# Strassen's seven products for 16 of the 22 blocks of the down projection, and 13 low halves moved to VectorE

## The chip, the core and the metric

One core of a Trainium2 chip runs the kernel: TensorE (PE) multiplies matrices into eight banks of PSUM, VectorE (DVE), ScalarE (ACT) and GpSimd (POOL) work elementwise, SyncE (SP) issues most of the loads. The metric is the time of one execution on the device in microseconds, the median of several runs. Lower is better.

## The reference

One layer of an encoder with 512 tokens, d_model 1024 and a feed-forward width of 2816, in float32. Two kinds of attention, gates, an output projection w_o and a residual come first; what the change touches is mostly the end:

```python
merged = g_a * (y_a @ w_up_a[l]) + g_b * (y_b @ w_up_b[l])
x = x + gate1[:, None] * (merged @ w_o[l])
h2 = rms_norm(x, norm2_g[l]) * (1.0 + scale2[:, None]) + shift2[:, None]
ff = (jax.nn.silu(h2 @ w_ff1[l]) * (h2 @ w_ff3[l])) @ w_ff2[l]
x = x + gate2[:, None] * ff
```

## The kernel before

**Precision.** Each float32 operand is split into a high half, rounded to the format that TensorE reads (`cp`, a cast on ScalarE, L432), and a low half, the difference (`sb` on VectorE, L456, or `psub` on POOL, L504). A product takes three matmuls: high by high, high by low, low by high (`three`, L519). A matmul has a stationary block of 128 x 128 and up to 512 moving columns.

**Weights** come in units of 128 x 1024 (512 KB): `g` (gates), `up`, `o` (w_o), `f1`, `f3` (one block of 128 columns of w_ff1 or w_ff3) and `f2` (128 rows of w_ff2). A unit is loaded into one of four `raw` buffers, cast into one of three `whi` buffers, and its low half goes into one of three `wlo`. A `raw` buffer is free again when the low half is formed, a `whi` and `wlo` when TensorE has used the unit. `take(u)` prepares units two ahead of the one used (LA = 2). The table `ON_DVE` says whose low halves VectorE forms; `g` and `up` units are not in it and go to POOL.

**Stages.** The units `g` and `up`, mixed with the attention, give the merged input of w_o, each of its eight blocks split into `mh` and `ml`; at the same time loads of the modulation weights (`in_adat`) are multiplied with the condition vector on VectorE (`raw<-raw,cs`, L476). Then come w_o, the second norm and 22 blocks of the feed-forward: for block j, f1 and f3 are multiplied with h2 (48 matmuls of 512 columns, blocks 0 and 1 in two parts), ScalarE takes silu of the one, VectorE multiplies by the other, and the result is split into `f` high and low. After that the 22 f2 units are multiplied into eight banks, `ob[t, h]` for four blocks of 128 tokens and two halves of the output columns: 16 units one after another, then the last six for one bank after the other, so that the outputs leave in turn. The last bank is done in two halves of 256 columns; the first 16 units of its second half are put aside in `first`.

**Order.** `Order.plan` lists every operation with its costs, buffers and priorities and writes out one fixed order for each engine; each engine then runs its instructions strictly in that order and waits on semaphores. A change of any part can move instructions elsewhere. The 36 tiles `t` of 512 columns hold the eight tiles of the residual (`x2`) and, before, the split blocks f.

## Time and profile before

| | us |
|---|---|
| median of 3 runs | 797.6 |
| lowest and highest | 796.84, 798.5 |
| the profiled execution | 797.95 |
| its span, first to last instruction | 795.7 |
| TensorE busy | 781.7 |
| VectorE, ScalarE, POOL busy | 459.3, 350.1, 178.1 |

The profiled execution's own time is 2.25 us more than its span, which lies around the instructions. Matmuls overlap at their ends, so a group's mean is longer than the time from one start to the next. Rows name L of the kernel that was run; an idle time stands in brackets, with what ended it.

### The profile page before, as it was taken

Reading aid. Unit: us, or ns where it says so; the run is one execution under the profiler, and the core shown is the slowest. Engines: PE = TensorE matmul, PEld = TensorE weight load, DVE = VectorE, ACT = ScalarE, POOL = GpSimd, SP = SyncE. Lnnn points to the kernel's source line nnn. Section 1 sums busy time; section 2 is a strip of 40 time slices with the busy share of each in tenths; the row PEclk is TensorE's granted clock in tenths of the full one; section 3 lists DMA queues with packets and bytes.
Section 4 is the critical chain, followed back from the end, with each engine's and each line's share of the span. In section 5 each row is a group of like instructions: output and inputs, shape, how many; then the busy total and the mean of one; then the engine's idle time right before and its main releaser. Section 6 shows DMA issues by size and latency. Waiting matters only on the chain.

```text
span 795.7 us, 11113 instructions
## 1 busy us (share of the span) xinstructions
PE 781.7 (98%) x4275; PEld 673.5 (85%) x4275; DVE 459.3 (58%) x911; ACT 350.1 (44%) x650; POOL 178.1 (22%) x115
## 2 busy tenths in 40 slices
PE   8999999999999999999899999999999999999998
PEld 5988988999899888888588988888888888888886
DVE  6969999765469886778746433443433333212343
ACT  6576575456568767525344332232332322211310
POOL 1056544786565313542001000000000000000000
PEclk9999999999999999999999999999999999999999
DMA  9932121222242333776602223444422232232311
GB/s 347 396 142 81 57 78 54 80 83 78 79 131 83 107 105 93 258 257 221 216 14 80 88 98 127 135 135 158 140 100 100 86 106 95 90 107 90 122 40 66
DMA packets 29147, 97.97 MB, mean 123 GB/s; under 512 B 3235, under 2 KB 4771, under 8 KB 29094
## 3 DMA queue, kind: packets, MB, share of 16 engines
q1 hardware_dynamic: 28518, 96.35, 35.3%
q10 hardware_dynamic: 576, 0.92, 0.3%
q8 instruction: 33, 0.54, 0.3%
q14 instruction: 20, 0.16, 0.1%
HBM read 95.16 MB, written 2.10 MB: 122 GB/s over the span
## 4 chain that ended last, share of the span: by engine, by line
PE 78%; DVE 12%; DMA 4%; ACT 3%; issue 2%; POOL 0%; SPq 0%; ACTq 0%; DVEq 0%; POOLq 0%
PE ff L519 45%; PE gate L519 6%; PE wo L519 4%; PE kb L519 3%; DMA raw<-in_adat 3%; PE qa L519 3%; PE ka L519 3%; DVE sc L878 2%; PE va L519 2%; PE qb L519 2%; PE S L519 2%; DVE m L877 2%; DVE raw L476 2%; PE PT L532 2%; PE idx L519 2%
## 5 line engine op out<-in xcount | busy, mean ns | idle before, releaser
L432 ACT CAST whi<-raw 128x1024 fp32r<-128x1024 f32 x109 | 114.5, 1052 | 279.8 <-PE ff L519 149.0
L456 DVE TENSOR_TENSOR wlo<-raw,whi 128x1024 fp32r<-128x1024 f32 x65 | 79.6, 1224 | 116.1 <-ACT whi L432 113.3
L504 POOL TENSOR_TENSOR wlo<-raw,whi 128x1024 fp32r<-128x1024 f32 x44 | 110.3, 2509 | 157.4 <-ACT whi L432 143.3
L519 PE MATMUL ff<-h2h,wlo 128*128 128x512 f32 (+1 forms) x384 | 142.6, 372 | 0.0
L519 PE MATMUL ff<-h2l,whi 128*128 128x512 f32 (+1 forms) x384 | 142.4, 371 | 0.0
L519 PE MATMUL ff<-h2h,whi 128*128 128x512 f32 (+1 forms) x384 | 142.4, 371 | 0.0
L519 PE MATMUL ff<-whi,f 128*128 128x512 f32 (+1 forms) x310 | 95.2, 385 | 0.0
L519 PEld LDWEIGHTS ff<-h2h,wlo 128*128 128x128 f32 x384 | 72.3, 188 | 12.6
L519 PEld LDWEIGHTS ff<-h2l,whi 128*128 128x128 f32 x384 | 72.3, 188 | 12.5
L519 PEld LDWEIGHTS ff<-h2h,whi 128*128 128x128 f32 x384 | 72.3, 188 | 12.4
L519 PEld LDWEIGHTS ff<-whi,f 128*128 128x128 f32 x310 | 57.9, 188 | 11.6
L519 PE MATMUL ff<-wlo,f 128*128 128x512 f32 (+1 forms) x155 | 59.7, 385 | 0.0
L462 DVE TENSOR_TENSOR silu<-ff,silu 128x512 f32<-128x512 f32 x22 | 15.2, 692 | 70.2 <-PE ff L519 70.2
L476 DVE CUSTOM_DVE_ANT_0 raw<-raw,cs 128x1024 f32<-128x1024 f32 x32 | 45.1, 1422 | 13.0 <-DMA raw<-in_adat 13.0
L519 PE MATMUL gate<-hl,whi 128*128 128x512 f32 x128 | 51.1, 399 | 0.0
L519 PE MATMUL gate<-hh,whi 128*128 128x512 f32 x128 | 51.0, 399 | 0.0
L519 PE MATMUL gate<-hh,wlo 128*128 128x512 f32 x128 | 51.0, 398 | 0.0
L485 POOL TENSOR_TENSOR r<-v,mhalf 128x16 f32<-128x16 f32 (+2 forms) x14 | 29.1, 2080 | 71.5 <-DVE v L466 71.1
L441 ACT ACTIVATE sx<-sx,nm 128x128 f32<-128x128 f32 (+3 forms) x64 | 35.7, 560 | 9.7 <-DVE nm L476 9.5
L519 PEld LDWEIGHTS ff<-wlo,f 128*128 128x128 f32 x155 | 29.1, 188 | 5.9
L519 PE MATMUL wo<-wo,mh 128*128 128x512 f32 x96 | 30.5, 395 | 3.4 <-ACT mh L432 3.4
L470 DVE SCALAR_TENSOR_TENSOR acc<-raw,csc,acc 128x1024 f32<-128x1024 f32 x16 | 20.5, 1279 | 21.3 <-DMA raw<-in_adar 21.2
(229 smaller groups left out, 1692.6 us busy)
## 6 DMA issues: line engine op xcount, KB each, us to landing
raw<-in_wun SPq DMA_DIRECT2D x118, 512.0 KB, 3.3
raw<-in_adat SPq DMA_DIRECT2D x32, 512.0 KB, 7.3
raw<-in_adar SPq DMA_DIRECT2D x16, 512.0 KB, 3.2
x<-in_x SPq DMA_DIRECT2D x4, 512.0 KB, 5.4
praw<-in_wun SPq DMA_DIRECT2D x8, 256.0 KB, 7.4
xr<-in_x SPq DMA_DIRECT2D x4, 512.0 KB, 5.1
praw<-in_wun SPq DMA_DIRECT2D x8, 162.0 KB, 7.4
out_y<-out SPq DMA_DIRECT2D x4, 256.0 KB, 2.0
```

The lines of the kernel that those rows point to most:

```text
L432: nc.scalar.copy(g(o), g(i))
L441: nc.scalar.activation(g(o), g(i), f, scale=g(scale), **kw)
L456: dve(n, False, lambda: nc.vector.tensor_sub(g(o), g(i), g(j)), (i, j), (o,), two=(i, j))
L462: dve(n, False, lambda: nc.vector.tensor_mul(g(o), g(i), g(j)), (i, j), (o,), two=(i, j))
L470: dve(n, False, lambda: nc.vector.scalar_tensor_tensor(g(o), g(i), g(s), g(j), op0=op0, op1=op1), (i, s, j), (o,), len(refs(s)), (i, j))
L476: dve(n, False, lambda: nc.vector.tensor_tensor_reduce(g(o), g(i), g(j), scale, init, op0, op1, g(acc)), (i, j), (o, acc), two=(i, j))
L485: G.op("POOL", 300 + 165 * m, lambda: nc.gpsimd.tensor_tensor(g(o), g(i), g(mhalf[:, 0:1].spread([P, m])), op=ALU.pow), refs(i, mhalf), re ...
L504: G.op("POOL", 147 + 2.106 * n, lambda: nc.gpsimd.tensor_sub(g(o.r()), g(i), g(hi)), (i, hi), (o,), port=True)
L519: lambda: nc.tensor.matmul(g(ap), g(lhsT.r()), g(rhs.r()), start=i == 0, stop=i == self.count - 1), refs(lhsT, rhs), (ap,))
L532: G.op("PE", 109, lambda: nc.tensor.transpose(g(ap), g(in_), g(idt)), refs(in_, idt), (ap,))
L877: dve(n, False, lambda: nc.vector.max(g(m8), g(s)), (s,), (m8,))
L878: dve(n, False, lambda: nc.vector.match_replace(g(s), g(m8), g(s), TAKEN), (m8, s), (s,))
```

## The change

With A the token half and k-half blocks of f, and B those of w_ff2, a pair of f2 units (256 rows) is a 2 x 2 block product, which takes eight block products. The new code takes seven (in Winograd's form) for eight pairs, k = 0 to 7, and leaves the last six units as they were. Each product has 256 tokens in two banks, 512 output columns, and an inner length of 128.

- Per pair the products of gate and up are stored by quadrant in `fz` and `fy`, and four sums (`form`) give `fn`, `fm` and a new half of `fy`. Of these `fz` and `fn` are split for the first pass (three pairs early, the others once ff1 and ff3 are done and their `h` tiles are free), `fy` and `fm` for the second.
- The first pass makes four products per pair in the banks a, b, c, d (24 matmuls), from the units `fe` and `fo`, on which three differences of 512 columns are formed first. At its end ScalarE copies a, and VectorE adds b, c and d into `uv` and `uw`.
- The second pass makes three products per pair in g, e, f (18 matmuls) from the unit `go`, which is loaded again, and `gt`, half a unit with one difference. ScalarE's casts for it wait for the copies of a (`after=(done,)`).
- Then the sums are multiplied by gate2 and added to `x2`; the banks g and e go on to collect the last six units, and two new banks replace the other two (`first` is gone).
- The low halves of the eight `up` units and of g 14, 7, 15, 4 and 6 move from POOL to VectorE (`ON_DVE`).

```diff
@@ the list of weight units
+    for k in range(NP):
+        u += [("fe", k), ("fo", k)]
+    for k in range(NP):
+        u += [("go", k), ("gt", k)]
+    u += [("f2", j) for j in range(2 * NP, 22)]
@@ what is packed for them
+        elif u[0] in ("fe", "fo", "go"):
+            j = 2 * u[1] + (u[0] != "fe")
+            w = f["w_ff2"][0][128 * j:128 * j + 128, :]
+        elif u[0] == "gt":
+            w = f["w_ff2"][0][256 * u[1]:256 * u[1] + 128, 512:]
@@ who takes the low halves (settings)
-ON_DVE = ('f1', 'f3', 'f2', 'p', 'o')
+ON_DVE = ('f1', 'f3', 'f2', 'p', 'o', 'up') + tuple(('g', j) for j in (14, 7, 15, 4, 6))
@@ in split
+        if u[0] in ("fe", "go"):
+            return
+        if u[0] == "fo":
+            e, o = raws.pop(("fe", u[1]))[0], raws.pop(u)[0]
+            (e0, e1), (o0, o1) = ([x[:, 512 * h:512 * h + 512].k(h) for h in range(2)] for x in (e, o))
+            sub(e1, e1, e0, 512)
+            sub(o1, o1, e1, 512)
+            sub(o0, o0, o1, 512)
+            for v, x in ((("fe", u[1]), e), (u, o)):
+                hi, lo = new("whi", "whi"), new("wlo", "wlo")
+                cp(hi, x, 1024)
+                sb(lo, x, hi, 1024)
+                splits[v] = (hi, lo)
+        if u[0] == "gt":
+            o, t = raws.pop(("go", u[1]))[0], raws.pop(u)[0][:, 0:512]
+            sub(t, o[:, 512:1024], t, 512)
+            for v, x, n in ((("go", u[1]), o, 1024), (u, t, 512)):
+                hi, lo = new("whi", "whi")[:, :n], new("wlo", "wlo")[:, :n]
+                cp(hi, x, n)
+                sb(lo, x, hi, n)
+                splits[v] = (hi, lo)
+            return
@@ ahead of the loop over j
+    fz = [new("t", "fz") for _ in range(NP)]
+    fy = [new("t", "fy") for _ in range(NP)]
+    fn = [new("t", "fn") for _ in range(NP)]
+    fm = [new("t", "fm") for _ in range((NP + 1) // 2)]
+    early = [("pt", "m"), ("m", "m"), ("t", "t")]
+    ftags = ["sx"] * (NSX // 2) + ["pt"] * (NPT - 1)
+    fa = {}
+    def form(k):
+        f11, f22 = (fz[k][:, 256 * h:256 * h + 256].k(h) for h in range(2))
+        f12, f21 = (fy[k][:, 256 * h:256 * h + 256].k(h) for h in range(2))
+        s1, s2 = (fn[k][:, 256 * h:256 * h + 256].k(h) for h in range(2))
+        c = 256 * (k % 2)
+        add(s1, f21, f22, 256)
+        sub(s2, s1, f11, 256)
+        sub(f21, f11, f21, 256)
+        sub(fm[k // 2][:, c:c + 256].k(k % 2), f12, s2, 256)
+    def parts(x, h, l, after=()):
+        act(h.r(), x, 512, after=after)
+        sb(l, x, h, 512)
+        return h, l
+    def split_first(k, his, los):
+        fa[k] = [parts(x, h, l) for x, h, l in zip((fz[k], fn[k]), his, los)]
@@ in the loop over j: gate, up, product
...
+        k = j // 2
+        if k >= NP:
+            mul(s, b3, s, 512)
+            h, l = pair(ftags[j - 2 * NP], "f")
+            cp(h, s, 512)
+            sb(l, s, h, 512)
+            fs[j] = (h, l)
+            continue
+        for h in range(2):
+            z = (fz if h == j % 2 else fy)[k]
+            c = slice(256 * h, 256 * h + 256)
+            mul(z[:, c].k(h), b3[:, c], s[:, c], 256)
+        if j % 2:
+            form(k)
+            if k < len(early):
+                split_first(k, *(pair(x, "fh") for x in early[k]))
@@ in place of 16 of the 22 f2 units
+    more = [x[:, i, :].k(i) for x in (new("h", "fh"), new("h", "fh")) for i in range(8)]
+    pa, pc = [Bank("ff2a") for _ in range(2)], [Bank("ff2c") for _ in range(2)]
+    pb, pd = [Bank("ff2b", "sb") for _ in range(2)], [Bank("ff2d", "tb") for _ in range(2)]
+    def prods(banks, hl_, c0, w, n0):
+        hi, lo = hl_
+        for i, b in enumerate(banks):
+            c = slice(c0 + i * P, c0 + i * P + P)
+            b.three(b, hi[:, c], lo[:, c], w[0][:, n0:n0 + 512], w[1][:, n0:n0 + 512], 512)
+    for k in range(NP):
+        we, wo_ = take(("fe", k)), take(("fo", k))
+        if len(early) <= k + FD < NP:
+            split_first(k + FD, (more.pop(0), more.pop(0)), (new("t", "fl"), new("t", "fl")))
+        z, n = fa[k]
+        todo = [(pa, z, 0, we, 0), (pc, n, 0, we, 512), (pb, n, 256, wo_, 512), (pd, z, 256, wo_, 0)]
+        if k == NP - 1:
+            todo[1:3] = todo[2:0:-1]
+        for x in todo:
+            prods(*x)
+    ue, uv, uw = [], [], []
+    for i in range(2):
+        e, v, w = new("t", "ue"), new("t", "uv"), new("t", "uw")
+        done = act(e, pa[i], 512)
+        add(v, pb[i], e, 512)
+        add(w, pc[i], v, 512)
+        add(v, pd[i], v, 512)
+        ue.append(e)
+        uv.append(v)
+        uw.append(w)
+    pg, pe, pf = [Bank("ff2g") for _ in range(2)], [Bank("ff2e") for _ in range(2)], [Bank("ff2f", "sb") for _ in range(2)]
+    for k in range(NP):
+        y = parts(fy[k], more.pop(0) if more else new("t", "fh"), new("t", "fl"), (done,))
+        if k % 2 == 0:
+            m = parts(fm[k // 2], new("t", "fh"), new("t", "fl"), (done,))
+        wo_, wt = take(("go", k)), take(("gt", k))
+        prods(pg, y, 0, wo_, 0)
+        prods(pe, m, 256 * (k % 2), wo_, 512)
+        prods(pf, y, 256, wt, 0)
+    ob = {}
+    def rest_of(u, t, h):
+        mul(u, u, accs[1][:, 512 * h:512 * h + 512], 512)
+        add(x2[t, h], u, x2[t, h], 512)
+    for i in range(2):
+        x = new("t", "ux")
+        add(x, pf[i], uw[i], 512)
+        add(uv[i], pf[i], uv[i], 512)
+        ob[i, 0], ob[i, 1], ob[2 + i, 0], ob[2 + i, 1] = pg[i], pe[i], Bank("ff2", "tb"), Bank("ff2", "sb")
+        for u, t, h in ((ue[i], i, 0), (uw[i], i, 1), (uv[i], 2 + i, 0), (x, 2 + i, 1)):
+            rest_of(u, t, h)
@@ the last half column block
                 if n0:
-                    first = new("s", "first")[:, 0:n]
-                    mul(first, b[:, c], gs, n)
-                    add(first, first, rest, n)
-                    b, c, rest = Bank("ff2"), slice(0, n), first
+                    b, c = Bank("ff2"), slice(0, n)
```

**VectorE's order in the first pass.** Before, a unit of f2 gave VectorE one low half `wlo` every 24 matmuls. Now one step of the pass stands like this (numbers tell buffers apart: `fz` and `fn` are what is split, raw_6712 and raw_6743 the units fe and fo of step 3, the next two those of step 4, then step 5):

```order
L466 TENSOR_TENSOR wlo_6804<-raw_6712,whi_6790 128x1024
L466 TENSOR_TENSOR raw_6772<-raw_6772 128x512
L466 TENSOR_TENSOR fl_6819<-fz_6043,fh_6692 128x512
L466 TENSOR_TENSOR wlo_6823<-raw_6743,whi_6812 128x1024
L466 TENSOR_TENSOR raw_6795<-raw_6795,raw_6772 128x512
L466 TENSOR_TENSOR fl_6838<-fn_6117,fh_6692 128x512
L466 TENSOR_TENSOR raw_6795<-raw_6795 128x512
L466 TENSOR_TENSOR wlo_6846<-raw_6772,whi_6835 128x1024
L466 TENSOR_TENSOR raw_6815<-raw_6815 128x512
L466 TENSOR_TENSOR fl_6861<-fz_6196,fh_6761 128x512
L466 TENSOR_TENSOR raw_6832<-raw_6832,raw_6815 128x512
L466 TENSOR_TENSOR wlo_6869<-raw_6795,whi_6857 128x1024
```

Between two low halves of weights now stand differences and low halves of `fz` and `fn`, in a row that waits in turn for loads (the differences), for casts (`wlo`) and for buffers.

**The change of passes, TensorE and VectorE.** TensorE, from the last matmul of the first short unit (whi_7037) of the second pass on; whi_6996 is the unit go of step 0, whi_7055 and whi_7095 are go and gt of step 1:

```order
L529 MATMUL ff2f_7082<-whi_7037,fl_7041 128x512
L529 MATMUL ff2g_7050<-whi_7055,fh_6761 128x512
L529 MATMUL ff2g_7050<-wlo_7069,fh_6761 128x512
L529 MATMUL ff2g_7053<-whi_7055,fh_6761 128x512
L529 MATMUL ff2g_7053<-wlo_7069,fh_6761 128x512
L529 MATMUL ff2f_7071<-whi_7095,fh_6761 128x512
L529 MATMUL ff2e_7065<-whi_6996,fl_7098 128x512
L529 MATMUL ff2e_7075<-whi_6996,fl_7098 128x512
L529 MATMUL ff2e_7065<-whi_7055,fh_7021 128x512
```

VectorE, from the first sum out of the banks b:

```order
L469 TENSOR_TENSOR uv_7015<-ff2b_6710,ue_7003 128x512
L466 TENSOR_TENSOR raw_6993<-raw_6974,raw_6993 128x512
L469 TENSOR_TENSOR uw_7028<-ff2c_6695,uv_7015 128x512
L469 TENSOR_TENSOR uv_7034<-ff2b_6719,ue_7009 128x512
L466 TENSOR_TENSOR fl_7041<-fy_5166,fh_6761 128x512
L466 TENSOR_TENSOR wlo_7048<-raw_6957,whi_7037 128x512
L469 TENSOR_TENSOR uv_7015<-ff2d_6726,uv_7015 128x512
L469 TENSOR_TENSOR uw_7063<-ff2c_6704,uv_7034 128x512
L466 TENSOR_TENSOR wlo_7069<-raw_6974,whi_7055 128x1024
L469 TENSOR_TENSOR uv_7034<-ff2d_6733,uv_7034 128x512
L466 TENSOR_TENSOR raw_7059<-raw_7018,raw_7059 128x512
L466 TENSOR_TENSOR fl_7098<-fm_5253,fh_7021 128x512
L466 TENSOR_TENSOR wlo_7103<-raw_6993,whi_7095 128x512
```

Matmuls of the two first steps are mixed, those that need `fl_7098`, the low half of `fm`, come late; VectorE's sums out of the banks stand between low halves of the weights. Before, eight banks simply went on.

**VectorE just before the last products with w_o.** Before, the end of the stretch (`wo` is a low half of w_o, `gate<-gate` the sum that gives a block of the merged input, `wlo_4627` the first f1 unit's):

```order
L456 TENSOR_TENSOR wo_4578<-raw_4530,wo_4564 128x512
L456 TENSOR_TENSOR wo_4585<-raw_4530,wo_4571 128x512
L459 TENSOR_TENSOR gate_4404<-gate_4404,gate_4137 128x512
L456 TENSOR_TENSOR wo_4600<-raw_4549,wo_4587 128x512
L456 TENSOR_TENSOR wo_4607<-raw_4549,wo_4591 128x512
L456 TENSOR_TENSOR ml_4613<-gate_4404,mh_4603 128x512
L462 TENSOR_TENSOR gate_4184<-up_4538,gate_4184 128x512
L462 TENSOR_TENSOR gate_4226<-up_4566,gate_4226 128x512
L456 TENSOR_TENSOR wlo_4627<-raw_4568,whi_4609 128x1024
L459 TENSOR_TENSOR gate_4184<-gate_4184,gate_4226 128x512
L456 TENSOR_TENSOR ml_4646<-gate_4184,mh_4642 128x512
```

And now:

```order
L466 TENSOR_TENSOR wo_4578<-raw_4526,wo_4560 128x512
L466 TENSOR_TENSOR wo_4589<-raw_4526,wo_4566 128x512
L466 TENSOR_TENSOR wo_4593<-raw_4543,wo_4580 128x512
L466 TENSOR_TENSOR wo_4601<-raw_4543,wo_4587 128x512
L469 TENSOR_TENSOR gate_4408<-gate_4408,gate_4144 128x512
L472 TENSOR_TENSOR gate_4188<-up_4539,gate_4188 128x512
L472 TENSOR_TENSOR gate_4230<-up_4568,gate_4230 128x512
L466 TENSOR_TENSOR ml_4623<-gate_4408,mh_4616 128x512
L469 TENSOR_TENSOR gate_4188<-gate_4188,gate_4230 128x512
L466 TENSOR_TENSOR wlo_4631<-raw_4570,whi_4606 128x1024
L466 TENSOR_TENSOR ml_4641<-gate_4188,mh_4634 128x512
L472 TENSOR_TENSOR x2_4652<-wo_4599,gbc_4111 128x512
```

The six low halves of w_o stand together, the sum of one block stands behind all of them, and the f1 unit's low half stands behind the last sum.

## Rows read from the trace of the kernel before

**Rows 1.** The page: busy time of TensorE, and the granted clock by slices.

```profile
PE 781.7 (98%) x4275; PEld 673.5 (85%) x4275; DVE 459.3 (58%) x911; ACT 350.1 (44%) x650; POOL 178.1 (22%) x115
...
PEclk9999999999999999999999999999999999999999
```

**Rows 2.** Windows: length, busy time of each engine (instructions), clock, DMA share, GB/s.

```profile
370.00:380.00 10.00, 9.62 (x43) 7.45 (x42) 9.97 (x15) 6.71 (x11) 0.00 (x0) 1.00 0.71 224
380.00:390.00 10.00, 6.41 (x26) 4.36 (x25) 8.16 (x13) 4.47 (x7) 0.00 (x0) 1.00 0.90 292
...
500.00:510.00 10.00, 10.00 (x46) 8.29 (x45) 4.30 (x5) 3.15 (x4) 0.00 (x0) 1.00 0.49 159
...
700.00:710.00 10.00, 10.00 (x46) 8.29 (x45) 2.45 (x2) 1.36 (x2) 0.00 (x0) 1.00 0.31 105
```

**Rows 3.** Timeline of ScalarE in the product with w_ff2.

```profile
704.69 1.05 ACT L432 CAST whi<-raw 128x1024 fp32r<-128x1024 f32 x1 [4.38 <-PE ff L519]
710.13 1.05 ACT L432 CAST whi<-raw 128x1024 fp32r<-128x1024 f32 x1 [4.38 <-PE ff L519]
```

**Rows 4.** Groups by form, 434 to 796 us, VectorE and ScalarE.

```profile
L456 DVE TENSOR_TENSOR wlo<-raw,whi 128x1024 fp32r<-128x1024 f32 x60 | 73.5, 1225 | 115.0 <-ACT whi L432 112.3
L456 DVE TENSOR_TENSOR f<-silu,f 128x512 fp32r<-128x512 f32 x22 | 15.0, 684 | 0.0
...
L432 ACT CAST f<-silu 128x512 fp32r<-128x512 f32 x22 | 13.7, 621 | 0.0
```

**Rows 5.** Timeline of VectorE: without a wait, and with one on the row ahead.

```profile
754.74 1.23 DVE L456 TENSOR_TENSOR wlo<-raw,whi 128x1024 fp32r<-128x1024 f32 x1 [3.01 <-ACT whi L432]
755.88 2.49 DVE L456 TENSOR_TENSOR f<-raw,f 128x512 fp32r<-128x512 f32 x4
...
787.65 0.69 DVE L462 TENSOR_TENSOR out<-ff,gbc 128x512 f32<-128x512 f32 x1 [2.66 <-PE ff L519]
788.38 0.69 DVE L459 TENSOR_TENSOR out<-out,x 128x512 f32<-128x512 f32 x1
```

**Rows 6.** The tile raw: loads, 690 to 800 us; then 300 to 390 us.

```profile
DMA to landing us min/median/max: 3.2/3.2/4.6
...
L476 DVE CUSTOM_DVE_ANT_0 raw<-raw,cs x16: 1210/1226/3433, 310.2 to 362.2; 128x1024 f32<-128x1024 f32 x16
L504 POOL TENSOR_TENSOR wlo<-raw,whi x12: 2388/2502/3187, 304.2 to 366.4; 128x1024 fp32r<-128x1024 f32 x12
...
DMA to landing us min/median/max: 3.2/4.5/6.6
```

**Rows 7.** Timeline of VectorE and POOL before w_o.

```profile
314.79 2.56 DVE L476 CUSTOM_DVE_ANT_0 raw<-raw,cs 128x1024 f32<-128x1024 f32 x1 [0.85 <-DMA raw<-in_adat]
...
358.83 3.43 DVE L476 CUSTOM_DVE_ANT_0 raw<-raw,cs 128x1024 f32<-128x1024 f32 x1 [0.49 <-DMA raw<-in_adat]
...
358.78 2.40 POOL L504 TENSOR_TENSOR wlo<-raw,whi 128x1024 fp32r<-128x1024 f32 x1 [2.77 <-ACT whi L432]
```

**Rows 8.** The chain of waits, 355 to 390 us: start, length, what.

```profile
353.79 5.02 DMA raw<-in_adat
...
363.88 5.29 DMA raw<-in_wun
...
377.84 4.49 DMA raw<-in_wun
...
387.91 0.63 ACT mh L432
```

**Rows 9.** Timeline of TensorE in the first products with w_o.

```profile
384.11 0.73 PE L519 MATMUL wo<-wo,mh 128*128 128x512 f32 x2 [1.73 <-ACT mh L432]
...
388.58 1.20 PE L519 MATMUL wo<-wo,mh 128*128 128x512 f32 x4 [1.70 <-ACT mh L432]
```

**Rows 10.** Windows around those two waits.

```profile
382.00:384.00 2.00, 0.38 (x2) 0.00 (x0) 1.76 (x4) 1.60 (x3) 0.00 (x0) 1.00 0.96 301
...
386.00:388.00 2.00, 0.88 (x4) 0.38 (x2) 1.88 (x3) 0.09 (x1) 0.00 (x0) 1.00 0.86 309
```

More of the change, by code (lines that the diff above doesn't have):

```diff
@@ L41 @@
 PROG = PROG.split()
+NP, FD = 8, 1
 def _units():
@@ L55, in _units @@
         u += [("f1", j), ("f3", j)]
-    u += [("f2", j) for j in range(22)]
+    for k in range(NP):
[3 more added lines that the diff above has]
+    u += [("f2", j) for j in range(2 * NP, 22)]
     return u
@@ L551, in load @@
         t = new("raw", "raw")
-        dma(t, a["wun"][UIX[u]], 512)
+        if u[0] == "gt":
+            dma(t[:, 0:512], a["wun"][UIX[u]][:, 0:512], 256)
+        else:
+            dma(t, a["wun"][UIX[u]], 512)
         raws[u] = (t, 1024)
@@ L1203, in _body @@
         act(s, b1, 512, AF.Silu)
-        mul(s, b3, s, 512)
-        h, l = pair(ftags[j], "f")
-        cp(h, s, 512)
-        sb(l, s, h, 512)
-        fs[j] = (h, l)
-    ob = {(t, h): Bank("ff2", ("mm", "mm", "sb", "tb")[t]) for t in range(NB) for h in range(2)}
-    NK = 16
-    for j in range(NK):
-        w = take(("f2", j))
-        for t in range(NB):
-            for h in range(2):
-                hs = slice(512 * h, 512 * h + 512)
-                ts_ = slice(t * P, (t + 1) * P)
-                ob[t, h].three(ob[t, h], fs[j][0][:, ts_], fs[j][1][:, ts_], w[0][:, hs], w[1][:, hs], 512)
+        k = j // 2
@@ new lines, in _body @@
+    ob = {}
[9 more added lines that the diff above has]
+            rest_of(u, t, h)
+    NK = 2 * NP
```

3 lines of the change are left out of this document (2 added, 1 removed).

## The prediction

> **What bounds the kernel now.** I read the page first, then the table of windows, the waits of TensorE, and the chain of waits. The reader is to see in the page that TensorE is busy for 781.7 of 795.7 us at a granted clock that never leaves its upper level, 2.4 GHz [rows 1]. So the time is TensorE's work plus its idle time, 14.0 us. The windows say where that idle time is: none in the feed-forward part (10.00 of 10 us in every window from 440 to 790; two stand here), 3.97 us between 370 and 390 us, just before and in the first products with w_o [rows 2]; the rest is the start, the tail behind the last matmul and crumbs. In the product with w_ff2 VectorE works 2.5 us in 10, so there is cover [rows 2].
>
> **The change, part by part.**
>
> *Matmuls removed.* Sixteen blocks took 16 x 8 x 3 = 384 matmuls of 512 columns. Now eight pairs take seven products of two banks and three matmuls, 8 x 42 = 336. The built order confirms it: 4262 matmul instructions before, 4214 now. One f2 unit is 24 matmuls, and ScalarE, which waits for one in each round, starts its cast at 704.69 and at 710.13 us [rows 3]: 5.44 us a unit, 226.7 ns a matmul. 48 x 0.2267 = **-10.9 us** if TensorE stays fed. Every matmul still loads its own stationary block, so I keep the pace.
>
> *Feeding the first pass.* A step (one pair, 24 matmuls, 5.44 us) needs on VectorE three differences of 512, two low halves of 1024 and, for steps 3 to 7, two low halves of 512 (the rows of VectorE's order in the first pass show such a step). Durations of one alone are 1225 and about 684 ns [rows 4]; but instructions that stand behind one another without a wait start every 1.14 us (754.74 to 755.88) and 0.60 us (four in 2.49), while one that needs the result just before it follows in 0.73 us [rows 5]. So 5 x 0.60 + 2 x 1.14 = 5.3 us back to back, 5.87 us alone, against TensorE's 5.44. Over the pass it is 8 steps x 5.44 = 43.5 us against, back to back, some 36 us (seven steps' weights at 4.1, ten halves of 0.6, one product of the last gate unit). I walked it through row by row in the order that stands. The three splitting buffers come free every half step, so a unit may be cast two half steps (5.44 us) before it is needed and takes some 2.3 us; a raw buffer comes round every two steps, 10.9 us, against 3.2 us of landing here [rows 6], 1.8 us of differences and 2.3 us of splitting. The tightest low halves are those of steps 4 to 6, ready 1.7 to 2.4 us early back to back, and within 0.2 us of too late with each instruction at its lone duration. If a load takes 4.5 us, the median of the stage from 300 to 390 us [rows 6], one low half is late by 0.4 us. Cost: 0 to 2.2 us (five steps at 0.43), I take **0.3**, since there is no POOL work here and most rows are independent of the row ahead. ScalarE needs 2 x 1.05 + 2 x 0.62 = 3.3 us of 5.44 [rows 3, 4].
>
> *The change of passes.* Call the end of the first pass 0. Its banks end in the order a (-4.1), b (-2.7), c (-1.4), d (0). ScalarE copies the two a banks by about -3.1 and then casts fy and fm; VectorE adds b, c and d into the sums between its splits. In the order rows, TensorE runs 20 matmuls (4.5 us) and then wants whi_7095, the second short unit. That cast needs the buffer of the first short unit, free after 16 matmuls (3.7 us), and stands on ScalarE behind five casts that end near 4.3; it ends near 4.9. Next come two matmuls that want fl_7098, which VectorE reaches after eleven instructions from -3.0, near 4.8. So TensorE waits about 0.5 us; with every VectorE and ScalarE row at its lone duration the same walk gives 2.1 us here and 1.2 us more in later steps. What would hide the first sum is the 36 matmuls that the first two steps mix; without that cover the whole lag is paid. I take **+0.7**, ends 0 and 3.3. From the third step VectorE needs 3.3 us a step against 18 x 0.2267 = 4.08: it gains.
>
> *The rest of the product.* The last six blocks (144 matmuls) and the tail keep their shape. What is new beside them, 20 sums and gate products (12 to 14 us on VectorE), lies under 32.6 us of matmuls; its last row stands 108 matmuls before the end. The last two halves lose their `first` pieces: the mul and add behind the last matmul stay as they are, so **0**.
>
> *The gate-up part (ff1, ff3).* VectorE gains some 4 us per pair of units (products in halves, four forms, two splits for the first three pairs, less two low halves) over 21.8 us of TensorE. It is busy for 4.3 us of 10 there [rows 2]. Cost nothing; without that cover, 4 us a pair.
>
> *Low halves moved to VectorE.* Thirteen of 2.4 to 3.2 us (median 2.5) [rows 6, 7] leave POOL; VectorE pays 13 x 1.14 to 1.22 = 15 to 16 us. Two things come back. While POOL works on one, VectorE's instructions stretch: beside POOL's row from 358.78 a product with the condition vector takes 3.43 us [rows 7], where the fastest of its kind takes 1.21 [rows 6]. Seven such stretches lie between 312 and 362 us, 11 us together (the first and the last stand in [rows 7]), and ten of the thirteen low halves: about even. And the buffers come free 1.2 to 2 us sooner. The chain of waits shows why that matters: load of the modulation weights, the stretched product, load of w_o, VectorE's queue, the last load of w_o, the cast mh, and only then TensorE at 388.6 [rows 8, 9]. TensorE's two waits there are 1.73 and 1.70 us, both for mh [rows 9]. In the built order VectorE's work from the first w_o low half to the last sum of `gate` is 24 rows of 512 and two of 1024, 16.8 us; before it was 23 and three, 17.3 us, with some 0.4 us of waits. The low half of the first f1 unit now stands behind that sum, and one gate product more ahead of it. With the w_o loads at the same times the gain is 0.2 us, with loads 2.2 us earlier (the one stretch on this chain) 2.4 us; all idle gone would be 4.0. A wlo of VectorE now stands in the same queue as products that wait for their loads; two pushed behind the sum cost 2.3 us. I take **-1.3**, ends -4.0 and +2.3.
>
> Sum: -10.9 + 0.3 + 0.7 - 1.3 = -11.2. The profiled execution took 797.95 us, 0.35 above the median of the three; on the median this is **786.4 us**.
>
> **A rule on the clock.** TensorE idled 1.6 us of one 2 us window and 1.1 of another between 382 and 388 us, and the granted clock stayed at 1.00, the level of 2.4 GHz [rows 10]. So waits of the size that I forecast cost their length alone. The Trainium skill ("TensorE: Matmul & The Clock Gate", section "HAM oscillation — how this bites in real kernels") warns that a kernel whose matmul groups are shorter than the waits between them is put back to the lower clock again and again. By the trace the sum stays 786.4; by that rule, were the waits at the change of passes long, it would be the third rival. No run here yet shows it.
>
> **Rivals.**
>
> 1. *VectorE falls behind in the product.* For it: 5.87 us a step at lone durations against 5.44, an order that is fixed, and casts that wait for buffers ahead of ready work. Against it: rows that run back to back at 0.60 and 1.14 [rows 5], and 7 us to spare over the pass. Price: 2.2 in the first pass and 3.3 behind it instead of 1.0: 790.9 us.
> 2. *The moved low halves hold up TensorE before w_o.* For it: VectorE is the engine that the chain names from 369 to 388 [rows 8]. Against it: the stretched rows go with POOL's work. Price: +2.3 instead of -1.3: 790.0 us.
> 3. *The clock falls at the change of passes (slower than before).* If TensorE starves there long enough to be granted 1.2 GHz, each matmul takes 226.7 ns more. It decides from 11.2/0.2267 = 50 matmuls at the low level; with the first half of the second pass (72 matmuls) in it, 786.4 + 16.3 = 802.7 us. Against it: the clock in [rows 10], and that no wait in my sum is longer than those.
>
> **Numbers.** Forecast (783.5 to 789): 0.62; rival 1 (789 to 794): 0.20; rival 2 (788.5 to 791.5): 0.11; rival 3: 0.03; something not seen: 0.04. The measurement tells differences of about 0.2%, 1.6 us. Range: the low end is the full removal of the idle time before w_o with no wait in the product, 797.6 - 10.9 - 4.0 = 782.7, rounded to 783 since both bounds together are unlikely; the high end takes in rivals 1 and 2 at their prices, 791. Faster by over 0.2%: 0.93 (the forecast, both first rivals, nothing else reaches back to 796); within: 0.03; slower: 0.04.
>
> **What would show it.** In the profile after: steps of 5.44 us between every second cast of whi in the first pass and 4.08 in the second; no TensorE wait over 0.5 us there but one near the twentieth matmul of the second pass, on ACT whi or DVE fl; VectorE above 80% busy in the first pass; loads landing in under 4.5 us; no low half on POOL after 280 us; the stretched rows of 3.4 us gone; the first full run of w_o matmuls starting before 388 us. I am wrong if TensorE waits for wlo or whi in every step, if the pace of a matmul is not 227 ns with stationary blocks from the forms, or if TensorE idles more than 4 us between 360 and 390 us.

## The result and the profile after

The changed kernel takes **787.2 us** (median of four runs, 785.55 to 788.77) against 797.4 for the kernel before, measured beside it: ratio 0.9863, 95% interval 0.9842 to 0.9885. Two later series with the same kernel, each beside the kernel before, gave 0.9873 (0.9852 to 0.9894) and 0.9871 (0.9852 to 0.9891). Forecast: 786.4, range 783 to 791.

The profiled execution is the slowest of the four: 788.77 us, span 787.0, 8.7 less than before. The first matmul of each stage, from the timeline of TensorE, says where this lies (one execution of each kernel, so the 0.50 us before w_o can be chance):

| stretch, from first matmul to first matmul | before, us | after, us | difference |
|---|---|---|---|
| start to the first product with w_o | 377.36 | 377.86 | +0.50 |
| w_o to the first product with w_ff1 | 51.67 | 50.63 | -1.04 |
| ff1 and ff3 | 242.83 | 242.85 | +0.02 |
| product with w_ff2 to its last matmul | 119.80 | 111.53 | -8.27 |
| tail | 4.05 | 4.13 | +0.08 |

Page, parts 1 and 2 (compare [rows 1]):

```profile
PE 772.5 (98%) x4227; PEld 665.0 (84%) x4227; DVE 529.4 (67%) x1056; ACT 370.7 (47%) x680; POOL 142.7 (18%) x102
PEclk9999999999999999999999999999999999999999
```

Windows of ten us, columns as in [rows 2], and two of one us:

```profile
380.00:390.00 10.00, 7.93 (x28) 5.47 (x26) 7.50 (x11) 3.22 (x5) 0.00 (x0) 0.83 0.78 271
386.00:387.00 1.00, 1.00 (x3) 0.81 (x3) 0.69 (x2) 0.00 (x0) 0.00 (x0) 0.50 0.08 20
387.00:388.00 1.00, 1.00 (x4) 0.71 (x4) 0.00 (x0) 0.00 (x0) 0.00 (x0) 0.50 0.72 188
680.00:690.00 10.00, 10.00 (x46) 8.29 (x45) 10.00 (x14) 4.15 (x5) 0.00 (x0) 1.00 0.61 206
700.00:710.00 10.00, 10.00 (x46) 8.29 (x45) 6.76 (x7) 3.50 (x4) 0.00 (x0) 1.00 0.52 172
710.00:720.00 10.00, 8.97 (x39) 6.78 (x38) 7.78 (x12) 8.96 (x16) 0.00 (x0) 1.00 0.32 107
```

The first pass has no gap: its 192 matmuls take 43.52 us, 226.7 ns each, though VectorE is busy in all of 680 to 690 and for 37.4 us of the 43.5. The second thing to see is the granted clock, 0.83 between 380 and 390 where it was 1.00 before: for about three of these microseconds it is 0.50, the level of 1.2 GHz. The page's row of slices does not show it, since a slice is 20 us long.

TensorE's timeline there answers to [rows 9]:

```profile
381.71 0.39 PE L529 MATMUL wo<-wo,ml 128*128 128x512 f32 x1
383.69 0.73 PE L529 MATMUL wo<-wo,mh 128*128 128x512 f32 x2 [1.59 <-ACT mh L442]
...
384.75 0.43 PE L529 MATMUL wo<-wo,mh 128*128 128x512 f32 x1
385.66 1.65 PE L529 MATMUL wo<-wo,mh 128*128 128x512 f32 x3 [0.48 <-ACT mh L442]
387.11 0.63 PE L529 MATMUL wo<-wo,ml 128*128 128x512 f32 x1
387.54 0.63 PE L529 MATMUL wo<-wo,mh 128*128 128x512 f32 x1
```

The idle time fell from 3.97 to 2.07 us, but from 385.66 to 388.39 six matmuls start 0.455 us apart on average instead of 0.227, and the one at 384.75 is slow too: about 1.6 us given back. The stretched products are gone, as forecast; the last low half on POOL starts at 304.2 us, where the forecast had none after 280. Rows of the tile `raw`, 300 to 400 us (compare [rows 6]), and of the line of `psub`:

```profile
L486 DVE CUSTOM_DVE_ANT_0 raw<-raw,cs x16: 1217/1226/1228, 310.6 to 359.3; 128x1024 f32<-128x1024 f32 x16
L514 POOL TENSOR_TENSOR wlo<-raw,whi x31: 2381/2402/2900, 47.5 to 304.2; 128x1024 fp32r<-128x1024 f32 x31
```

The change of passes, first on TensorE, then on VectorE:

```profile
715.08 0.39 PE L529 MATMUL ff2g<-wlo,fh 128*128 128x512 f32 x1
715.31 0.39 PE L529 MATMUL ff2g<-whi,fh 128*128 128x512 f32 x1
716.59 0.50 PE L529 MATMUL ff2g<-whi,fl 128*128 128x512 f32 x1 [0.89 <-DVE fl L466]
```

```profile
711.89 0.68 DVE L469 TENSOR_TENSOR uv<-ff2b,ue 128x512 f32<-128x512 f32 x1
714.05 0.69 DVE L466 TENSOR_TENSOR raw<-raw 128x512 f32<-128x512 f32 x1 [1.48 <-DMA raw<-in_wun]
714.65 0.68 DVE L469 TENSOR_TENSOR uw<-ff2c,uv 128x512 f32<-128x512 f32 x1
715.26 0.68 DVE L469 TENSOR_TENSOR uv<-ff2b,ue 128x512 f32<-128x512 f32 x1
715.85 0.68 DVE L466 TENSOR_TENSOR fl<-fy,fh 128x512 fp32r<-128x512 f32 x1
```

TensorE waits for `fl` at the fourth matmul of the pass. VectorE could have formed it from 712.2 us on (ScalarE's cast stands at 711.57), but ahead of it in the queue is the difference of `go` 1 and `gt` 1, which waits 1.48 us for its load. With smaller gaps behind it, this change of passes costs 1.78 us.

Before the last six units it is ScalarE's queue, in the same way: a cast waits 1.20 us for the load of the twentieth unit, and behind it stands the cast of the nineteenth, which TensorE needs first.

```profile
750.44 0.62 ACT L442 CAST f<-raw 128x512 fp32r<-128x512 f32 x1 [1.20 <-DMA raw<-in_wun]
750.97 1.05 ACT L442 CAST whi<-raw 128x1024 fp32r<-128x1024 f32 x1
```

```profile
752.07 0.50 PE L529 MATMUL ff2g<-whi,f 128*128 128x512 f32 x1 [0.29 <-ACT whi L442]
```

Below, "excess" is the sum, over the product with w_ff2, of what matmuls start later than 0.2267 us after the one before them, where they start more than 0.3 us after it: 2.45 us in this profile, 1.78 of it at the change of passes and 0.67 before the last six units.

### The profile page after: what moved, and what is told of

Read it like the earlier page. It is cut to its first block, busy times and chain, and to the rows that moved or that the text cites. A ratio compares the mean times of both kernels' runs of the same rounds, so it can differ in the third digit from the quotient of the medians.

```text
span 787.0 us, 11241 instructions
## 1 busy us (share of the span) xinstructions
PE 772.5 (98%) x4227; PEld 665.0 (84%) x4227; DVE 529.4 (67%) x1056; ACT 370.7 (47%) x680; POOL 142.7 (18%) x102
## 4 chain that ended last, share of the span: by engine, by line
PE 68%; DVE 16%; DMA 8%; ACT 4%; issue 3%; POOL 0%; SPq 0%; POOLq 0%; DVEq 0%; ACTq 0%
PE ff L529 32%; PE gate L529 5%; PE wo L529 4%; DMA raw<-in_adat 4%; DMA raw<-in_wun 3%; PE kb L529 3%; PE qa L529 3%; PE ka L529 3%; DVE wlo L466 3%; DVE sc L914 2%; PE va L529 2%; DVE m L913 2%; PE S L529 2%; PE PT L542 2%; PE qb L529 2%
## 5 line engine op out<-in xcount | busy, mean ns | idle before, releaser
L442 ACT CAST whi<-raw 128x1024 fp32r<-128x1024 f32 x125 | 127.8, 1024 | 250.9 <-PE ff L529 127.4
L466 DVE TENSOR_TENSOR wlo<-raw,whi 128x1024 fp32r<-128x1024 f32 (+1 forms) x94 | 110.3, 1175 | 42.6 <-ACT whi L442 41.3
L514 POOL TENSOR_TENSOR wlo<-raw,whi 128x1024 fp32r<-128x1024 f32 x31 | 75.0, 2419 | 129.4 <-ACT whi L442 125.0
L486 DVE CUSTOM_DVE_ANT_0 raw<-raw,cs 128x1024 f32<-128x1024 f32 x32 | 38.7, 1221 | 8.5 <-DMA raw<-in_adat 8.2
L529 PE MATMUL S<-qk 128*128 128x128 f32 (+3 forms) x128 | 29.3, 333 | 1.1 <-DVE nm L486 1.1
L466 DVE TENSOR_TENSOR raw<-raw 128x512 f32<-128x512 f32 x32 | 21.9, 686 | 10.4 <-DMA raw<-in_wun 10.4
L529 PEld LDWEIGHTS gate<-hh,whi 128*128 128x128 f32 x128 | 24.1, 188 | 4.4
L529 PEld LDWEIGHTS gate<-hl,whi 128*128 128x128 f32 x128 | 24.1, 188 | 4.3
L529 PEld LDWEIGHTS gate<-hh,wlo 128*128 128x128 f32 x128 | 24.1, 188 | 4.3
```

The source lines that it names most:

```text
L442: nc.scalar.copy(g(o), g(i))
L466: dve(n, False, lambda: nc.vector.tensor_sub(g(o), g(i), g(j)), (i, j), (o,), two=(i, j))
L486: dve(n, False, lambda: nc.vector.tensor_tensor_reduce(g(o), g(i), g(j), scale, init, op0, op1, g(acc)), (i, j), (o, acc), two=(i, j))
L514: G.op("POOL", 147 + 2.106 * n, lambda: nc.gpsimd.tensor_sub(g(o.r()), g(i), g(hi)), (i, hi), (o,), port=True)
L529: lambda: nc.tensor.matmul(g(ap), g(lhsT.r()), g(rhs.r()), start=i == 0, stop=i == self.count - 1), refs(lhsT, rhs), (ap,))
```

## Experiments

### The two halves of the change by themselves

`strassen_alone`:

```diff
-ON_DVE = ('f1', 'f3', 'f2', 'p', 'o', 'up') + tuple(('g', j) for j in (14, 7, 15, 4, 6))
+ON_DVE = ('f1', 'f3', 'f2', 'p', 'o')
```

> The changed kernel with the low halves of up and the five gate units back on POOL. Theory (the 48 matmuls are the gain, the moved low halves about 1 us of it): from the first to the last matmul with w_ff2 111.5 us as in the changed kernel; before the products with w_o two waits of some 1.7 us for mh at clock 1.00 as in the kernel before; time 797.4 - 8.3 - 0.1 = 789.0 us (788.2 to 789.8). Rival A (the moved low halves are worth nothing, since the clock took back what the waits gave): 787.2 us or less. Rival B (the moved low halves carry more than 2 us): above 790.

`move_alone` is the kernel before with the longer `ON_DVE`.

> The kernel before with the low halves of up and the five gate units on VectorE, and no Strassen. Theory: idle time between 380 and 390 us from 4.0 to about 2.1 us, the stretched products of 3.4 us gone; 797.4 - 1.0 = 796.4 us if the clock falls to 0.50 for 3 us there, 794.6 us if it stays at 1.00. Rival (the move does nothing by itself, VectorE's queue holds TensorE up instead): 797.4 us or more, with idle time still near 4 us.

Measured: `strassen_alone` 789.55 us, ratio 0.9892 (0.9871 to 0.9913): -8.6 us of 798.5. `move_alone` 796.24, ratio 0.9974 (0.9960 to 0.9988): -2.1 us. Together -10.7, about what the changed kernel has (-9.9 to -10.2). The product took 111.17 us in `strassen_alone`, with the same wait of 0.8 us for `fl`. `strassen_alone` had waits of 0.59 and then 1.69 us for mh at clock 1.00; `move_alone` 0.64 and 0.52, also at 1.00, less than the 2.1 us of its theory, and its profiled execution took 794.74 us, as that theory has it for clock 1.00 (794.6). Rival A (the move is worth nothing) is not supported: against the changed kernel measured beside it (788.38) `strassen_alone` is 1.2 us longer, though their runs overlap, and `move_alone` alone has an interval clear of 1.

### The wait before w_o and the clock

`again` and `third_time` are the changed kernel unaltered; `fill_wait` and `wo_mix` give TensorE work in the place of the wait.

> The changed kernel once more, unaltered. Theory (the pattern of waits before the products with w_o brings the clock down): median between 786 and 788.5 us, and the profile shows the granted clock at 0.50 again for some 3 us from about 385 us, behind a wait of 1.6 us for mh and a second of 0.5. Rival (the fall was chance): the clock stays at 1.00 there in this profile, the first full run of products with w_o starts some 1.8 us earlier, and the profiled execution is nearer 785.5 than 788.8.

> The changed kernel unaltered, as the reference of this call. Theory (the length of the waits for mh before w_o differs from one execution to the next with the landing of the loads of w_o, and the clock falls where the wait is 1.6 us or more): ratio to the kernel before 0.985 to 0.9885; the profile has either a wait of 1.6 us or more and a granted clock of 0.50 behind it, or waits under 1.2 us and a clock of 1.00. Rival (the clock has nothing to do with the waits): a long wait at clock 1.00 throughout, or a short one with 0.50 behind it.

```diff
# fill_wait, in the loop over k, ahead of k = 6 for t = h = 0
+    fill = Bank("fill", "tb")
+    for _ in range(7):
+        ... nc.tensor.matmul(fill, merged[5][0][:, 0:P], ohl[5, 0][0], start=True, stop=True)
```

> The changed kernel with seven matmuls of 512 columns, whose results nobody reads, on TensorE between the products with the sixth and the seventh block of merged for the first bank, where TensorE waits 1.6 us for mh. Theory (the idle time brings the clock down): the granted clock stays at 1.00 from 380 to 395 us, the matmuls behind the wait come every 0.227 us instead of 0.43, and the time is 1.8 us below the changed kernel: 785.4 us. Rival (the fall has another cause, or TensorE's clock is not what counts there because ScalarE's mh ends later anyway): 787.2 us, or up to 788 where the seven matmuls end after mh.

```diff
# wo_mix
+    for t in range(2):
+        wo_part(t, 0, 0, 6)          # k = 0 to 5 of the banks (0, 0) and (1, 0)
     for t in range(NB):
         for h in range(2):
-            b = Bank("wo", "mm")
-            for k in range(8): ...
+            wo_part(t, h, 6 if (t, h) in bank_of else 0, 8)
+            b = bank_of[t, h]
```

> The changed kernel with the products with w_o in another order: the first six blocks of merged for the first two banks come ahead of the seventh and eighth, so that TensorE has 18 matmuls (4.1 us) of its own work where it waited 1.6 and 0.5 us for mh. Theory (idle time there costs its length, and the clock that falls behind it 1.8 us more): no wait over 0.3 us there, clock 1.00, from the first product with w_o to the first with w_ff1 48.0 to 48.6 us instead of 50.6 to 51.5; time 2.5 to 3.3 us below the changed kernel. Rival (the norm behind the first bank comes later, so that TensorE waits at the first products with w_ff1 instead): the gain is under 1 us, with a wait on h2h or xm near 426 us.

Measured: `again` 788.38 us, `third_time` 788.34, `fill_wait` 786.36 (0.9854, 0.9832 to 0.9877), 2.0 below `again` with overlapping intervals, where 1.8 was forecast, `wo_mix` **783.82** (0.9806, 0.9780 to 0.9832). What the profiles show between 377 and 430 us, and, in the last column, what every execution on record adds: in how many its mean granted clock was 0.998 or less. In the profiles that goes with a fall before w_o (all four at 0.998 or less had it, none of the ten at 0.999 or 1.000):

| kernel | waits for mh, us | granted clock behind them | first w_o to first w_ff1, us | executions with mean clock 0.998 or less |
|---|---|---|---|---|
| changed | 1.59, 0.48 | 0.50 | 50.63 | 2 of 4 |
| again | 2.60, 0.27 | 0.50 | 51.52 | 6 of 6 |
| third_time | 2.93 | 0.50 | 52.65 | 5 of 6 |
| product_fixes (below) | 2.62, 0.52 | 0.50 | 52.03 | 2 of 5 |
| six_pairs (below) | 1.72, 0.52 | 1.00 | 49.49 | 3 of 5 |
| vector_dose (below) | 1.15, 0.52 | 1.00 | 48.91 | 2 of 6 |
| y_first (below) | 0.53 | 1.00 | 47.75 | 3 of 5 |
| strassen_alone | 0.59, 1.69 | 1.00 | 49.74 | 2 of 6 |
| move_alone | 0.64, 0.52 | 1.00 | 48.45 | 5 of 12 |
| fill_wait | none | 1.00 | 48.00, of it 1.59 the seven | 0 of 5 |
| wo_mix | none | 1.00 | 46.43 | 0 of 5 |

TensorE in `third_time`, in `six_pairs` and in `fill_wait`:

```profile
384.80 1.22 PE L529 MATMUL wo<-wo,mh 128*128 128x512 f32 x2 [2.93 <-ACT mh L442]
...
386.25 2.18 PE L529 MATMUL wo<-wo,mh 128*128 128x512 f32 x4
```

```profile
383.62 0.73 PE L529 MATMUL wo<-wo,mh 128*128 128x512 f32 x2 [1.72 <-ACT mh L442]
...
385.60 0.96 PE L529 MATMUL wo<-wo,mh 128*128 128x512 f32 x3 [0.52 <-ACT mh L442]
```

```profile
382.20 1.75 PE L1178 MATMUL fill<-wo,mh 128*128 128x512 f32 x7
383.79 0.62 PE L529 MATMUL wo<-wo,mh 128*128 128x512 f32 x2
384.24 0.39 PE L529 MATMUL wo<-wo,ml 128*128 128x512 f32 x1
384.47 1.07 PE L529 MATMUL wo<-wo,mh 128*128 128x512 f32 x4
```

Four things follow. First, the four matmuls behind the wait take 2.18 us in `third_time` and 1.07 in `fill_wait`: the clock's part of the cost is real, and without the wait it is not paid. Second, the first seven kernels of the table have one and the same order of instructions in this stretch, yet their waits run from 0.53 to 2.93 us and the stretch from 47.75 to 52.65: it differs from execution to execution, and is wide enough to hold the spread of the runs (785.55 to 789.28 us in all three series). Third, in these profiles waits of 2.6 us and more were always followed by 0.50, waits of 1.15 and less never; 1.6 to 1.7 us came out both ways (three profiles at 1.00, that of before [rows 9, 10] among them, one at 0.50). So the claim of `third_time` that 1.6 us brings the clock down holds only in part. Fourth, with work in the place of the wait no execution shows the fall (0 of 10 in `fill_wait` and `wo_mix`), where the changed kernel has it in 13 of its 16: these took 788.3 us in the mean, the other three 786.0. The kernel before has it in 12 of the 46 executions measured beside the experiments, 800.0 us against 798.0. That the move of the low halves makes the fall more frequent is not shown: 2 of 6 without it, in `strassen_alone`, are too few.

`wo_mix` beats its own forecast of 2.5 to 3.3: some 5 us less by its ratio, since the stretch that it replaces is longer in the other two profiles of the changed kernel (51.5, 52.7) than in the one that I worked from (50.6). Its profile has neither wait nor a lower clock; the rival (a later wait at w_ff1) did not come:

```profile
384.00:386.00 2.00, 2.00 (x10) 1.65 (x10) 2.00 (x4) 0.62 (x1) 0.00 (x0) 1.00 0.60 240
386.00:388.00 2.00, 2.00 (x11) 1.65 (x10) 1.15 (x2) 0.00 (x0) 0.00 (x0) 1.00 0.51 141
```

Why mh comes at different times is seen on ScalarE, first `y_first` with the short wait, then `third_time` with the long one:

```profile
380.14 1.05 ACT L442 CAST whi<-raw 128x1024 fp32r<-128x1024 f32 x1 [1.44 <-DMA raw<-in_wun]
381.09 0.61 ACT L442 CAST mh<-gate 128x512 fp32r<-128x512 f32 x1
```

```profile
383.18 1.05 ACT L442 CAST whi<-raw 128x1024 fp32r<-128x1024 f32 x1 [1.42 <-DMA raw<-in_wun]
384.13 0.61 ACT L442 CAST mh<-gate 128x512 fp32r<-128x512 f32 x1
```

The cast of the first f1 unit waits for its load and stands ahead of mh; the whole train of loads is 3 us later in the one than in the other. The traces say where the two part: the next to last load of modulation weights (`in_adat`) lands at 355.2 us in `y_first`, at 357.0 to 357.5 in the three kernels of this order with waits of 1.15 to 1.72 us, and at 358.2 to 358.6 in the three with 2.6 to 2.9; in all seven the next load is issued 1.3 us behind it. Why that load lands late was not tried.

### The waits in the product

```diff
# y_first
-        y = parts(fy[k], ...)
+        with G.moved(-500 if k == 0 else 0):
+            y = parts(fy[k], ...)
# product_fixes: this, and the casts of unit 19 and later ordered behind that of unit 18
-                cp(hi[h], t[:, 512 * h:512 * h + 512], 512)
+                act(hi[h].r(), t[:, 512 * h:512 * h + 512], 512, after=cast18)
```

> The changed kernel with one low half (fl of the first fy) ahead of the difference of two loads, and of three sums and differences, in VectorE's order at the change of passes. Theory (TensorE waits there because VectorE's queue stands 1.5 us before a load that nothing needs yet): the wait of 0.9 to 1.1 us on fl is gone, TensorE's excess between the last matmul of the first pass and 8 us later falls from 1.75 to under 0.8 us, and the time is 1.0 us below the changed kernel. Rival (the weights of the last six blocks come by a chain of loads of their own): the wait on fl goes, one of the same size on whi before the last six blocks grows from 0.3 to some 1.3 us, and from the first to the last matmul of the product it still takes 111 to 111.5 us: time as the changed kernel.

> The same, and ScalarE casts the nineteenth block of w_ff2 (whi) ahead of the twentieth, whose load comes later. Theory (both waits are instructions that stand in a queue behind one that waits for a load): both waits under 0.3 us, from the first to the last matmul of the product 109.2 to 109.8 us instead of 111.5; time 1.7 to 2.0 us below the changed kernel. Rival (the loads themselves are late, in whatever order the casts stand): the wait stays on whi or wlo, 110.5 us or more, gain under 0.7 us.

Measured: `y_first` 786.71 us, 0.9843 (0.9817 to 0.9870); `product_fixes` 786.35, 0.9849 (0.9823 to 0.9874). In `y_first` VectorE forms `fl` ahead of the difference, and TensorE does not wait for it; seven matmuls later it waits for one of the sums, which still stands behind that difference:

```profile
709.32 0.68 DVE L466 TENSOR_TENSOR fl<-fy,fh 128x512 fp32r<-128x512 f32 x1
710.49 0.69 DVE L466 TENSOR_TENSOR raw<-raw 128x512 f32<-128x512 f32 x1 [0.49 <-DMA raw<-in_wun]
```

```profile
711.92 0.39 PE L529 MATMUL ff2g<-wlo,fh 128*128 128x512 f32 x1
712.14 0.39 PE L529 MATMUL ff2g<-whi,fl 128*128 128x512 f32 x1
...
714.24 0.50 PE L529 MATMUL ff2e<-whi,fh 128*128 128x512 f32 x1 [0.35 <-DVE uw L469]
```

The excess at this change of passes is 0.80 us, the product 110.35, and the wait for `whi` did not grow (0.11 us), so the theory (under 0.8) is met only just, and the rival (111 to 111.5) not. By itself this run does not show the cause, since here VectorE waited only 0.49 us for the load: in `again`, with the old order and a wait of 0.50, TensorE did not wait for `fl` either, and the excess there was 0.72. What shows it is the six profiles with the old order. VectorE's wait at the difference was 1.48 and 1.35 us in the changed kernel and `strassen_alone`, and TensorE's for `fl` 0.89 and 0.78; it was 0.50 or nothing in `again`, `third_time`, `fill_wait` and `wo_mix`, and TensorE's nothing.

In `product_fixes` the nineteenth unit's cast comes first, and the excess is 0.43 us, the product 109.49:

```profile
749.86 1.06 ACT L442 CAST whi<-raw 128x1024 fp32r<-128x1024 f32 x1 [0.30 <-PE ff2f L529]
750.82 2.31 ACT L442 CAST f<-raw 128x512 fp32r<-128x512 f32 x4
```

Before the last six units too the wait follows the load. ScalarE's wait there was 2.69 us in `fill_wait`, 1.20 in the changed kernel, 1.06 and 1.04 in `strassen_alone` and `again`, 0.79 and 0.47 in `third_time` and `wo_mix`; TensorE's for `whi` 1.77, 0.29, 0.16, 0.14 and twice nothing, and nothing in the three profiles with the cast ahead. The longest, in `fill_wait`:

```profile
748.08 0.62 ACT L442 CAST f<-raw 128x512 fp32r<-128x512 f32 x1 [2.69 <-DMA raw<-in_wun]
```

But the size forecast for these two is not shown in the times. The unaltered order had an excess of 2.45, 1.21 and 0.74 us in its three profiles (product 111.53, 110.34, 109.87), and 2.09, 2.25 and 0.64 in `strassen_alone`, `fill_wait` and `wo_mix`: mean 1.56 us. The waits are there only when the load is late. Against the 0.43 of `product_fixes` the fixes would be worth about 1.1 us on average, within the uncertainty of these ratios; but at the change of passes the load was hardly late in any of the three profiles with both fixes (0.19, 0 and 0 us), so not all of this need be theirs.

### How near VectorE is to its limit, and fewer pairs

```diff
# vector_dose: 16 results that are not read
-            sub(o0, o0, o1, 512)
+            sub(o0, o0, o1, 512), [sub(new('s', 'dose'), e1, e0, 512) for _ in range(2)]
# six_pairs
-NP, FD = 8, 1
+NP, FD = 6, 1
+    for j in range(2 * NP, 16):      # ahead of the last six, with ob[t, h] as in the kernel before
+        ...
```

> The changed kernel with two differences of 512 columns more on VectorE in each of the eight steps of the first pass (their results are not read): 16 times 0.60 us, 9.6 us. Theory (VectorE just keeps up, with 5.3 us a step against TensorE's 5.44 and some 7 us to spare over the pass): a step takes 6.5 us on VectorE, the first pass grows by 2.6 us (what exceeds the spare) to 5.3 us (five steps at 1.06), with TensorE waiting on wlo; time 2.6 to 5.3 us above the changed kernel. Rival (VectorE is far from the bound there): under 1 us.

> The changed kernel with Strassen's products for six pairs of blocks instead of eight; the four blocks that this leaves run as three plain products per bank, ahead of the last six. Theory (a pair is worth six matmuls of 0.2267 us, whatever the number of pairs, and the change of passes costs the same): 12 matmuls more, product 2.7 us longer, time 2.0 to 3.5 us above the changed kernel of the same call. Rival A (most of the gain does not come from the matmuls): within 1 us of it. Rival B (the first pass was just fed, and every pair that is taken away gives VectorE time back): less than 1.5 us longer.

In `six_pairs` the four plain units run in full, but the output leaves out what they add to the last 256 columns of the last 128 rows.

Measured: `vector_dose` 788.18 us, 0.9869 (0.9845 to 0.9894), as the changed kernel; `six_pairs` 789.45, 0.9881 (0.9862 to 0.9901), 1.1 us above `third_time`, with overlapping runs. Windows and the one wait of the first pass in `vector_dose`:

```profile
680.00:690.00 10.00, 10.00 (x46) 8.29 (x45) 9.99 (x14) 4.22 (x4) 0.00 (x0) 1.00 0.56 189
690.00:700.00 10.00, 10.00 (x46) 8.28 (x45) 10.00 (x14) 3.48 (x4) 0.00 (x0) 1.00 0.63 209
700.00:710.00 10.00, 8.88 (x40) 6.99 (x39) 9.15 (x14) 3.22 (x4) 0.00 (x0) 1.00 0.41 133
```

```profile
707.07 0.73 PE L529 MATMUL ff2a<-whi,fl 128*128 128x512 f32 x2 [1.12 <-DVE fl L466]
```

With 9.6 us more, VectorE is busy without a break for 39 us (669.8 to 708.8), and TensorE waits for the first time 37.6 us into the pass: it ends 1.45 us later (44.97 for 43.52), and 1.2 us follows at the change of passes. So about 8 us were spare (9.6 - 1.45), near the 7 that the expectation worked with; the 1.45 lies between theory and rival. The median agrees with the rival, but only 2 of these 6 executions had the fall of the clock; the four without it took 788.0 us in the mean, 2.0 more than the three of the changed kernel.

`six_pairs` falls short of the 2.0 to 3.5 forecast: its 12 more matmuls are 2.7 us, but its profile has no excess at all (product 111.83 us for 492 matmuls), where eight pairs had 1.56 on average; 2.7 - 1.56 = 1.1. So the change of passes did not cost the same, and rival B's figure (less than 1.5 us) is met, though not its reason: in the first pass eight pairs had no wait either, and `vector_dose` shows 8 us to spare there. In the trace a pair's six matmuls are worth their 1.36 us, less what the waits for loads take back; that the times agree to 0.1 us is luck, as is seen from their spread (787.45 to 789.87 against 785.90 to 789.28).

### All together, and the moved low halves once more

`all_three` is `wo_mix` with both fixes of the product; `three_on_pool` is the same with the shorter `ON_DVE` of `strassen_alone`.

> The changed kernel with the order of the first products with w_o (wo_mix), the first low half of fy ahead (y_first), and the nineteenth block cast ahead of the twentieth (product_fixes). Theory (the idle time before w_o with the clock behind it, and the two waits in the product, add up): from the first product with w_o to the first with w_ff1 46.4 us, from the first to the last matmul of the product 109.3 to 109.8 us, time 5.5 to 6.5 us below the changed kernel of the same call. Rival (wo_mix took the product's waits with it already, since its profile shows the product in 109.8 us): 5 us or less, as wo_mix.

> The kernel of all_three with the low halves of up and the five gate units back on POOL. Theory (the moved low halves only shorten TensorE's waits for mh before w_o; where 18 matmuls lie in front of these waits, nothing is left to shorten): no wait over 0.5 us there, from the first product with w_o to the first with w_ff1 46.4 to 46.9 us, ratio to the kernel before as all_three, 0.9812, within 0.001. Rival (the instructions of VectorE that stretch beside POOL's cost time elsewhere too, or mh comes later than 4 us): 1 us or more above all_three, ratio 0.9825 or more.

Measured: `all_three` **783.35 us**, 0.9812 (0.9792 to 0.9832), 5.0 below `third_time`, measured beside it, and no run of the one reaches the other (782.48 to 783.81 against 785.90 to 789.28). w_o takes 46.43 us, the product 109.22 with 0.11 of excess. In time it is not told apart from `wo_mix`, so the rival holds: the fixes of the product add nothing that these runs can show. It is the fastest version here, 15 us below the kernel before, measured beside it.

`three_on_pool` 786.94 us, 0.9857 (0.9828 to 0.9886): its rival was right, and my theory wrong. Mh comes later than the 18 matmuls can cover (the last one is cast at 389.4, in `all_three` at 383.7), w_o takes 49.27 us, and the stretched products are back ahead of it:

```profile
355.80 3.17 DVE L486 CUSTOM_DVE_ANT_0 raw<-raw,cs 128x1024 f32<-128x1024 f32 x1 [0.16 <-DMA raw<-in_adat]
359.70 3.42 DVE L486 CUSTOM_DVE_ANT_0 raw<-raw,cs 128x1024 f32<-128x1024 f32 x1
```

```profile
390.06 0.73 PE L529 MATMUL wo<-wo,mh 128*128 128x512 f32 x2 [1.46 <-ACT mh L442]
```

## Why the prediction was right, by its steps

**Matmuls removed, -10.9.** Right: the pace is 226.7 ns with stationary blocks from the forms too. With 0.11 us of excess the product takes 109.22 us (`all_three`) against 119.80: -10.6.

**Feeding the first pass, +0.3.** It cost nothing: no wait at all in the profile; VectorE had some 8 us to spare (`vector_dose`), as the walk said. Of rival 1's price the 2.2 us of the first pass occurred in no profile of this order.

**Change of passes, +0.7.** The size was too low in this profile (1.78), near the mean of the six with this order (0.78), and that by luck, since the place was wrong: the fourth matmul, not the twentieth. The step that failed is the walk of VectorE's order "from -3.0": it counted the instructions back to back and did not ask which one in the queue would hold up the rest if its load came later. Where no load was late, the walk was right: in `third_time` the low half of `fm` ends 4.85 us behind the end of the first pass (forecast 4.8), with an excess of 0.22. The waits of VectorE and TensorE in the six profiles show that the late load is the cause.

**The rest of the product, 0.** Wrong by 0.67 us here, 2.1 in `fill_wait`, 0.78 in the mean, by the same mechanism on ScalarE, as the waits for the twentieth unit's load show. The terms for the product were +1.0 together, the mean over six profiles is 1.56.

**Low halves moved, -1.3.** By the medians right in size: `move_alone` -2.1 (-1.0 to -3.2 by its interval), and -1.2 by `strassen_alone` against `again`. The way was only half right. Idle time fell by 1.9 us, near the 2.4 given for earlier loads, but the step "waits of the size that I forecast cost their length alone" failed: the clock fell behind them. The rule of the Trainium skill ("TensorE: Matmul & The Clock Gate", section "HAM oscillation — how this bites in real kernels"), that groups of matmuls shorter than the waits between them bring the clock down, was weighed for the change of passes, where nothing of the kind is seen (0.9 us, clock 1.00). In the kernel that the Trainium skill tells it of, waits of some 3 to 5 us stand between groups of some 2 us. Before w_o here a wait of 1.59 us, then matmuls for about 1.5 us, then 0.48 more was followed by 0.50, though the waits are shorter than there, and `six_pairs` with 1.72 and 0.52 kept 1.00: the rule would not have told the two apart. The windows of [rows 10] are one execution that kept its clock, and I took it for the rule of that place.

**Sum.** -11.2 forecast, -10.2 measured in the first series (-10.1 and -9.9 in the other two). That it comes so near is in part luck, as executions of one clock show. Those without the fall (mean clock 0.999 or 1.000) took in the mean 798.0 us before (34 executions), 789.0 in `strassen_alone` (4), 795.4 in `move_alone` (7) and 786.0 changed (3): -9.0 or -9.4 for the products, as 10.9 less the mean excess of 1.56 has it, and -2.6 or -3.0 for the low halves, twice the term. Together -12.0. The fall, which the forecast put at nothing, then takes an estimated 1.4 us off the gain (13/16 of 2.4 us in the changed kernel, less 12/46 of 2.0 before; the 2.4 contain the longer wait). So two terms were too small in opposite directions. The means are of few executions and of different series, and not good to a few tenths.
